# Moving rows between ScalarE and VectorE at the end of a load-bound clamp-and-sum kernel

## The chip, the cores and the metric

One core of a Trainium2 chip. The time of a kernel is the device time of one execution in microseconds (us); medians of several executions are given. Every execution also has a *span*: from the first to the last instruction that the profile records.

## The reference

```python
# x: (32, 512, 1024) float32
def reference(x):
    relu_x = np.maximum(x, 0)
    return np.sum(relu_x, axis=-1).astype(np.float32)
```

It reads 67.1 MB and writes 64 KB.

## The kernel before

The input is 16,384 rows of 1024 numbers, or 128 rows on each of the 128 partitions. It is loaded in seven blocks of 16 rows per partition, then 8, 4, 2 and 1 rows, and the last row in four pieces. Three buffers take turns. SyncE issues all loads on one queue. A row can be done in two ways:

- in two steps: ScalarE clamps several rows in one instruction in place, VectorE sums them in one instruction (`TWO` lists the group sizes of each block);
- whole: one engine clamps and sums one row (`ACT` and `DVE` count such rows). A whole row takes *two* hardware instructions, the work and a read of the accumulator.

```python
TWO = [[16], [16], [16], [8, 8], [8, 8], [6, 5], []]
ACT = [0, 0, 0, 0, 0, 5, 8]
DVE = [0, 0, 0, 0, 0, 0, 8]
TAIL = [8, 4, 2, 1]
PIECES = [244, 252, 260, 268]
# ...
    for j in range(NB):                       # the seven blocks
        buf = bufs[j % NBUF]
        loaded = load(buf[:, :, :], rows(m, ROWS), j >= NBUF and freed[j - NBUF])
        # ... clamp and total for n in TWO[j]; act_row x ACT[j]; dve_row x DVE[j]
        freed.append((n_act, n_dve))
    # the tail of 8, 4, 2, 1 rows goes into the buffer of the fifth block
    # ...
    for n in TAIL:
        loaded = load(buf[:, c : c + n, :], rows(m, n), None if c else freed[NB - NBUF])
        for i in range(n):
            if i % 2 == 0:
                act_row(buf[:, c, :], m, loaded if i == 0 else None)
            else:
                dve_row(buf[:, c, :], res[:, m : m + 1], loaded if i == 1 else None)
            # ...
    # ... then the four pieces of the last row on VectorE, and the stores
```

## Time and profile before

| | before |
|---|---|
| time, median of 3 | 163.16 us (163.13 to 163.45) |
| span of the profiled run | 160.7 us |
| that run's time less its span | 2.44 us |
| load queue, share of 16 engines' span | 97.6% |
| last piece of the input begins to be summed | 158.04 us |

The first fence holds the page's lines on the span, on busy time with instruction counts (x), and on the load queue (packets, MB, share of 16 DMA engines).

```profile
span 160.7 us, 162 instructions
## 1 busy us (share of the span) xinstructions
DVE 117.0 (73%) x47; ACT 102.8 (64%) x52; POOL 0.2 (0%) x4
...
q1 hardware_dynamic: 2592, 67.18, 97.6%
...
```

The queue is busy 97.6% of the span, while no compute engine is over 73%. The same in stretches of the run (columns: stretch, its length, busy time of VectorE, ScalarE and GpSimd with instruction counts, clock, DMA share, GB/s):

```profile
...
41.30:60.60 19.30, 17.18 (x2) 13.85 (x1) 0.00 (x0) 1.00 1.01 435
60.60:80.00 19.40, 17.26 (x2) 13.86 (x1) 0.00 (x0) 1.00 1.00 432
80.00:99.30 19.30, 19.30 (x2) 13.95 (x2) 0.00 (x0) 1.00 1.00 435
...
156.80:160.70 3.90, 1.63 (x8) 0.80 (x2) 0.00 (x0) 1.00 0.17 38
...
```

In full blocks the loads move 432 to 435 GB/s. The upper figure equals the fabric ceiling that the Trainium skill gives under "DMA: Bandwidth & Descriptors", Specifications, so moving rows between engines was not expected to hurry the stream. The last stretch, 3.9 us, holds the last of the pieces (38 GB/s over 3.9 us, about 0.15 MB) and what follows the stream.

The chain that ended last (start, length, what):

```profile
...
74.54 51.60 DVE res L119 x5
...
127.97 28.83 DMA piece<-in_x_dram
...
156.82 1.20 DVE piece L136 x6
...
158.04 0.44 DVE piece L204
...
```

The chain goes through 51.6 us of VectorE's sums, because they free the buffer that the tail is loaded into. This can be read as a trap. The loads that were released at 126 us stand in the queue behind a block that lands only at 138 us, and their data arrives in its turn; releasing them a little sooner or later should change nothing. The end of the chain is real: the last piece's data, then 0.44 us of VectorE, then a store.

VectorE's timeline of the tail (start, length, instruction, and in brackets the idle time before it and what ended it) shows the landings, because VectorE starts at 147.77 and 152.67 when a load lands:

```profile
...
138.06 1.22 DVE L136 TENSOR_SCALAR_CACHE_REDUCE io<-io 128x1024 f32<-128x1024 f32 x1
...
147.77 1.22 DVE L136 TENSOR_SCALAR_CACHE_REDUCE io<-io 128x1024 f32<-128x1024 f32 x1 [0.51 <-DMA io<-in_x_dram]
...
152.67 1.22 DVE L136 TENSOR_SCALAR_CACHE_REDUCE io<-io 128x1024 f32<-128x1024 f32 x1 [0.25 <-DMA io<-in_x_dram]
...
155.15 1.22 DVE L136 TENSOR_SCALAR_CACHE_REDUCE io<-io 128x1024 f32<-128x1024 f32 x1
...
156.82 0.41 DVE L136 TENSOR_SCALAR_CACHE_REDUCE piece<-piece 128x244 f32<-128x244 f32 x1 [0.44 <-DMA piece<-in_x_dram]
...
158.04 0.44 DVE L204 TENSOR_SCALAR_CACHE_REDUCE piece<-piece 128x271 f32<-128x271 f32 x1
...
```

Last, the groups by shape, from which the change is costed (busy time, then mean ns of one):

```profile
...
L119 DVE TENSOR_REDUCE res<-io 128x6 f32<-128x6144 f32 x1 | 6.5, 6546 | 0.0
L119 DVE TENSOR_REDUCE res<-io 128x5 f32<-128x5120 f32 x1 | 5.5, 5480 | 0.0
L111 ACT ACTIVATE io<-io 128x6144 f32<-128x6144 f32 x1 | 5.3, 5322 | 5.4 <-DMA io<-in_x_dram 5.4
L111 ACT ACTIVATE io<-io 128x5120 f32<-128x5120 f32 x1 | 4.5, 4453 | 0.0
...
L136 DVE DVE_READ_ACCUMULATOR io<-io 128x1 f32 x15 | 1.2, 82 | 0.0
...
```

One row costs 1066 ns in a sum, 6546 - 5480, and 869 ns in a clamp, 5322 - 4453. A whole row takes 1.14 us from start to start on VectorE, 1.04 us on ScalarE.

### The profile page before, as it was taken

Reading aid. Unit: us, or ns where it says so; the run is one execution under the profiler, and the core shown is the slowest. Engines: PE = TensorE matmul, PEld = TensorE weight load, DVE = VectorE, ACT = ScalarE, POOL = GpSimd, SP = SyncE. Lnnn points to the kernel's source line nnn. Section 1 sums busy time; section 2 is a strip of 40 time slices with the busy share of each in tenths; the row PEclk is TensorE's granted clock in tenths of the full one; section 3 lists DMA queues with packets and bytes.
Section 4 is the critical chain, followed back from the end, with each engine's and each line's share of the span. In section 5 each row is a group of like instructions: output and inputs, shape, how many; then the busy total and the mean of one; then the engine's idle time right before and its main releaser. Section 6 shows DMA issues by size and latency. Waiting matters only on the chain.

```text
span 160.7 us, 162 instructions
## 1 busy us (share of the span) xinstructions
DVE 117.0 (73%) x47; ACT 102.8 (64%) x52; POOL 0.2 (0%) x4
## 2 busy tenths in 40 slices
DVE  0000000009999499994999999999999999998984
ACT  3000059990799709995099932999249992696882
POOL 0000000000000000000000000000000000000000
DMA  7996996996996996996996996996996997998992
GB/s 261 522 522 261 522 522 261 522 522 261 522 522 261 522 522 261 522 506 277 522 489 294 522 489 294 522 489 294 522 489 294 522 440 343 392 481 371 424 389 47
DMA packets 2592, 67.18 MB, mean 418 GB/s; under 512 B 672, under 2 KB 1184, under 8 KB 1312
## 3 DMA queue, kind: packets, MB, share of 16 engines
q1 hardware_dynamic: 2592, 67.18, 97.6%
HBM read 67.11 MB, written 0.07 MB: 418 GB/s over the span
## 4 chain that ended last, share of the span: by engine, by line
DMA 43%; DVE 33%; ACT 17%; another core or an unknown queue 3%; SPq 1%; issue 0%; DVEq 0%
DVE res L119 32%; DMA io<-in_x_dram 25%; DMA piece<-in_x_dram 18%; ACT io L111 17%; SPq L93 1%; DVE piece L136 1%; DVE piece L204 0%; DVEq L29 0%
## 5 line engine op out<-in xcount | busy, mean ns | idle before, releaser
L119 DVE TENSOR_REDUCE res<-io 128x8 f32<-128x8192 f32 (+3 forms) x9 | 97.9, 10933 | 40.1 <-ACT io L111 40.1
L111 ACT ACTIVATE io<-io 128x8192 f32<-128x8192 f32 (+3 forms) x9 | 79.2, 8826 | 47.2 <-DMA io<-in_x_dram 47.2
L126 ACT ACTIVATE io<-io 128x1024 f32<-128x1024 f32 x21 | 21.9, 1044 | 6.8 <-DMA io<-in_x_dram 6.8
L136 DVE TENSOR_SCALAR_CACHE_REDUCE io<-io 128x1024 f32<-128x1024 f32 x15 | 17.4, 1215 | 0.9 <-DMA io<-in_x_dram 0.8
L126 ACT ACTIVATION_READ_ACCUMULATOR io<-io 128x1 f32 x21 | 3.9, 187 | 0.0
L111 ACT ACT_TABLE_LOAD x1 | 1.3, 1283 | 0.8 <-PEq L249 0.8
L136 DVE TENSOR_SCALAR_CACHE_REDUCE piece<-piece 128x244 f32<-128x244 f32 (+2 forms) x3 | 1.2, 416 | 0.4 <-DMA piece<-in_x_dram 0.4
L136 DVE DVE_READ_ACCUMULATOR io<-io 128x1 f32 x15 | 1.2, 82 | 0.0
L204 DVE TENSOR_SCALAR_CACHE_REDUCE piece<-piece 128x271 f32<-128x271 f32 x1 | 0.4, 436 | 0.0
L136 DVE DVE_READ_ACCUMULATOR piece<-piece 128x1 f32 x3 | 0.2, 82 | 0.0
L249 POOL MEMSET const-bfloat16-1.0<- 128x1 bf16 x1 | 0.1, 102 | 0.0
L249 POOL MEMSET const-uint8-127<- 128x1 uint8 x1 | 0.1, 101 | 0.0
L249 POOL MEMSET const-float32-0.0<- 128x1 f32 x1 | 0.1, 99 | 0.2 <-issue 0.2
L249 POOL MEMSET const-float32-1.0<- 128x1 f32 x1 | 0.1, 98 | 0.0
L204 DVE DVE_READ_ACCUMULATOR piece<-piece 128x1 f32 x1 | 0.1, 84 | 0.0
## 6 DMA issues: line engine op xcount, KB each, us to landing
io<-in_x_dram SPq DMA_DIRECT2D x1, 4096.0 KB, 21.6
io<-in_x_dram SPq DMA_DIRECT2D x1, 2048.0 KB, 26.1
io<-in_x_dram SPq DMA_DIRECT2D x1, 1024.0 KB, 28.1
io<-in_x_dram SPq DMA_DIRECT2D x1, 512.0 KB, 28.9
piece<-in_x_dram SPq DMA_DIRECT2D x1, 134.0 KB, 28.4
piece<-in_x_dram SPq DMA_DIRECT2D x1, 130.0 KB, 28.6
piece<-in_x_dram SPq DMA_DIRECT2D x1, 126.0 KB, 28.7
piece<-in_x_dram SPq DMA_DIRECT2D x1, 122.0 KB, 28.8
```

Of the source, the lines that this page charges most:

```text
L93: dma = nc.sync.dma_start(out=dst, in_=src)
L111: i = nc.scalar.activation(out=ap, in_=ap, func=RELU)
L119: nc.vector.tensor_reduce(out=res[:, m : m + n], in_=ap, axis=mybir.AxisListType.X, op=ADD).wait_op(sems.act, n_act, "sem-ge").then_inc(se ...
L126: i = nc.scalar.activation(out=ap, in_=ap, func=RELU, accum_out=res[:, m : m + 1])
L136: i = nc.vector.tensor_scalar(out=ap, in0=ap, scalar1=0.0, scalar2=None, op0=MAX, op1=ADD, accum_out=accum_out,)
L204: nc.vector.tensor_scalar(out=last[:, :], in0=last[:, :], scalar1=0.0, scalar2=None, op0=MAX, op1=ADD, accum_out=res[:, NT - 1 : NT],).wai ...
L249: nc = _bacc.Bacc("TRN2", target_bir_lowering=False, num_devices=1)
```

## The change

Its intent is to use ScalarE's and VectorE's idle time near the end in another proportion. The sixth block becomes 7 + 7 rows in two steps and 2 rows on ScalarE (was 6 + 5 and 5). Of the seventh, ScalarE takes 9 rows and VectorE 7 (was 8 and 8). Of the tail's eight rows ScalarE takes 5 and VectorE 3 (was 4 and 4). No load, store, buffer or release changes.

```diff
-TWO = [[16], [16], [16], [8, 8], [8, 8], [6, 5], []]
-ACT = [0, 0, 0, 0, 0, 5, 8]
-DVE = [0, 0, 0, 0, 0, 0, 8]
+TWO = [[16], [16], [16], [8, 8], [8, 8], [7, 7], []]
+ACT = [0, 0, 0, 0, 0, 2, 9]
+DVE = [0, 0, 0, 0, 0, 0, 7]
@@
-            if i % 2 == 0:
+            if i % 2 == 0 or (n == 8 and i == 7):
                 act_row(buf[:, c, :], m, loaded if i == 0 else None)
```

## The prediction

> **What bounds the kernel.** The stream of loads. The queue table gives q1 97.6% of 16 engines' span. The stage windows give 435 GB/s in the stretches 41.3 to 60.6 us and 80.0 to 99.3 us, and the timeline shows each full block (8.4 MB) landing 19.36 us after the one before: 99.34, 118.70, 138.06 us. The last nine loads then land in order of issue: 8 rows at 147.77, 4 at 152.67, 2 at 155.15, 1 at 156.45, pieces from 156.8. That 435 equals the fabric ceiling in the Trainium skill, "DMA: Bandwidth & Descriptors", Specifications; this trace agrees. After the last landing come four short VectorE instructions on the pieces (156.82 to 158.48) and a store of 1.4 us.
>
> The chain of waits names VectorE's sums for 33% and ScalarE's clamps for 17%. I read this as an artefact: those sums release buffers, but the queue never ran dry. The eight-row load was issued at about 126.2 us, when the previous block had 12 us of transfer left.
>
> **What changes.** Sixth block: 11 rows clamped and summed plus 5 whole rows on ScalarE become 14 plus 2. Seventh: ScalarE 8 to 9 rows, VectorE 8 to 7. In the next eight rows: ScalarE 4 to 5, VectorE 4 to 3. No load, store, buffer or release changes: the last buffer that is used again is freed by the fifth block's sums, which are untouched. The queue's instruction list is the same.
>
> **Costs, from the groups by shape.** Sums: 6546 ns for 6 rows and 5480 for 5, so 1066 per row and an estimated 7.61 us for 7. Clamps: 5322 and 4453, so about 6.18 us for 7. A whole row takes 1.14 us start to start on VectorE and 1.04 on ScalarE.
>
> VectorE: sums start at 126.04 as before; two of 7 rows end near 141.2 instead of 137.98. It meets the seventh block 3.1 us late; seven rows end near 149.1 (147.3 before), so it is 1.3 us late for the eight rows that land at 147.77. Three rows there end at about 152.5 to 152.6, just ahead of the landing at 152.67. Caught up, by some 0.1 us.
>
> ScalarE: its clamps and two rows end near 133.1, ahead of the landing at 138.06. Nine rows end near 147.5, before 147.77. Five rows end near 153.0, 0.3 us late for the four-row load, two more near 155.15: caught up.
>
> Busy time should be VectorE 117.0 to about 117.6 us and ScalarE 102.8 to about 104.1. Nothing on the path of load stream, last piece and last store changes.
>
> **Prediction.** 163.15 us, 8 in 10 between 162.8 and 163.5. Faster by over 2%: 1%; within 2%: 98%; slower: 1%.
>
> **What the profile would show.** Right: landings at 138.06, 147.77, 152.67, 155.15, 156.45 and 156.8 within 0.1 us; queue share near 97.6%; VectorE without idle time from 74.5 us until about 152.5 us, its first row of the seventh block near 141.1; ScalarE idle from 133.1 to 138.06; first piece at 156.82 and the span near 160.7.
> Wrong: the pieces' sums starting later than their landing (VectorE's debt not paid); or landings that shift (engine work affects the transfers).
>
> **What would make it wrong.** VectorE's debt when the four-row load lands would have to exceed about 0.6 us (its idle time after that: 0.2 + 0.4) to reach the pieces: sums or rows slower than measured here. So would another rate of the loads; nothing here points to it.

## The result, and the profile after

The median fell to 162.59 us (162.49 to 162.68, 4 runs), beside 163.14 for the kernel before in the same comparison. The ratio is 0.9964, with a 95% interval of 0.9946 to 0.9981. Ratios are the mean time of one kernel's runs over that of the other's of the same rounds, so not quite the ratio of the medians. So it is a gain of about a third of a per cent: within 2%, as forecast, but outside the range of 162.8 to 163.5, and clear of noise.

The page of the kernel after:

```profile
span 160.7 us, 156 instructions
## 1 busy us (share of the span) xinstructions
DVE 117.7 (73%) x43; ACT 104.2 (65%) x50; POOL 0.2 (0%) x4
...
q1 hardware_dynamic: 2592, 67.18, 97.5%
...
```

The span is 160.7 us again, to the digit, with the same queue share. The instruction counts fell: 162 to 156 in all, VectorE 47 to 43, ScalarE 52 to 50. The chain:

```profile
...
74.57 51.60 DVE res L119 x5
...
128.01 28.82 DMA piece<-in_x_dram
...
156.86 1.15 DVE piece L136 x6
...
158.06 0.43 DVE piece L204
...
```

The same chain with the same lengths. VectorE's timeline:

```profile
...
141.13 1.21 DVE L136 TENSOR_SCALAR_CACHE_REDUCE io<-io 128x1024 f32<-128x1024 f32 x1
...
149.11 1.21 DVE L136 TENSOR_SCALAR_CACHE_REDUCE io<-io 128x1024 f32<-128x1024 f32 x1
...
152.53 0.08 DVE L136 DVE_READ_ACCUMULATOR io<-io 128x1 f32 x1
152.70 1.22 DVE L136 TENSOR_SCALAR_CACHE_REDUCE io<-io 128x1024 f32<-128x1024 f32 x1
...
155.19 1.22 DVE L136 TENSOR_SCALAR_CACHE_REDUCE io<-io 128x1024 f32<-128x1024 f32 x1
...
156.86 0.41 DVE L136 TENSOR_SCALAR_CACHE_REDUCE piece<-piece 128x244 f32<-128x244 f32 x1 [0.43 <-DMA piece<-in_x_dram]
...
158.06 0.43 DVE L204 TENSOR_SCALAR_CACHE_REDUCE piece<-piece 128x271 f32<-128x271 f32 x1
...
```

VectorE comes to the seventh block at 141.13 instead of 138.06, is late for the eight rows of the tail (149.11 instead of 147.77), has caught up at 152.70, and meets the pieces at 156.86 as before (156.82). Everything the prediction said of the span happened. And yet the time is 0.5 us shorter. Where is it?

Each execution has its own time and span. Time less span was 2.44 us in the profiled run of before, and 1.92 to 1.99 us (mean 1.96) in the four runs of after. So nearly the whole difference lies *outside the span*: after the last instruction that the profile records, or before the first.

One more thing differs in the trace. Besides the loads and stores it holds some DMA records of the kind "instruction", 8192 bytes each. The trace's page does not list them; these, read from the kept trace itself, are the records, with start times from the span's start:

```
8192-byte records of kind "instruction", profiled runs (start in us, from the span's start)
before  -11.03 -10.98 -10.82 -9.34 -8.42 -8.35 -8.13   and 162.81 (2.11 us after the span's end)
after   -11.02  -9.10  -8.40 -8.39 -8.30
```

I take such a record for the fetch of a block of instructions; the trace gives only its kind and size. The kernel before has one 2.1 us after its span, the kernel after has none. This gave the theory to test.

### The profile page after: what moved, and what is told of

The parts are those of the page before. It is cut to its first block, busy times and chain, and to the rows that moved or that the text cites. A ratio compares the mean times of both kernels' runs of the same rounds, so it can differ in the third digit from the quotient of the medians. Undisturbed runs are those within 1.5% of the kernel's fastest.

```text
span 160.7 us, 156 instructions
## 1 busy us (share of the span) xinstructions
DVE 117.7 (73%) x43; ACT 104.2 (65%) x50; POOL 0.2 (0%) x4
## 3 DMA queue, kind: packets, MB, share of 16 engines
q1 hardware_dynamic: 2592, 67.18, 97.5%
## 4 chain that ended last, share of the span: by engine, by line
DMA 43%; DVE 33%; ACT 17%; another core or an unknown queue 3%; SPq 1%; issue 0%; DVEq 0%
DVE res L119 32%; DMA io<-in_x_dram 25%; DMA piece<-in_x_dram 18%; ACT io L111 17%; SPq L93 1%; DVE piece L136 1%; DVE piece L204 0%; DVEq L29 0%
## 5 line engine op out<-in xcount | busy, mean ns | idle before, releaser
L119 DVE TENSOR_REDUCE res<-io 128x8 f32<-128x8192 f32 (+2 forms) x9 | 101.1, 11287 | 40.1 <-ACT io L111 40.1
L111 ACT ACTIVATE io<-io 128x8192 f32<-128x8192 f32 (+2 forms) x9 | 81.7, 9110 | 47.2 <-DMA io<-in_x_dram 47.2
L126 ACT ACTIVATE io<-io 128x1024 f32<-128x1024 f32 x20 | 20.8, 1043 | 5.4 <-DMA io<-in_x_dram 5.3
L136 DVE TENSOR_SCALAR_CACHE_REDUCE io<-io 128x1024 f32<-128x1024 f32 x13 | 15.0, 1214 | 0.2
```

What stands on the lines that cost most here:

```text
L111: i = nc.scalar.activation(out=ap, in_=ap, func=RELU)
L119: nc.vector.tensor_reduce(out=res[:, m : m + n], in_=ap, axis=mybir.AxisListType.X, op=ADD).wait_op(sems.act, n_act, "sem-ge").then_inc(se ...
L126: i = nc.scalar.activation(out=ap, in_=ap, func=RELU, accum_out=res[:, m : m + 1])
L136: i = nc.vector.tensor_scalar(out=ap, in0=ap, scalar1=0.0, scalar2=None, op0=MAX, op1=ADD, accum_out=accum_out,)
```

## Experiments

**Theories.** *Lengths*: the time outside the span depends on how many instructions ScalarE's and VectorE's streams hold, whatever they do. *Division* (the rival): it is the new division of rows among the engines. *Build*: each build of a program, or each chip, falls where it falls, and the 0.5 us is luck. The texts before each run use letters: A and V are *Lengths* of ScalarE's stream alone and of VectorE's alone, L of both together; S and W are *Division*; N is *Build*; B and C, explained where they come up, are two ideas of how the lengths act.

Stream lengths below are counted in the compiled programs (in every run 4 more for each of the two engines than its trace lists), and are written (ScalarE, VectorE): the kernel before is (62, 58), after is (60, 54). Streams were lengthened with drains, instructions that do no work, at the head of an engine's list, where ScalarE waits 19.9 us and VectorE 35.8 us for the first data:

```diff
+    for _ in range(2):
+        nc.scalar.drain()
+    for _ in range(4):
+        nc.vector.drain()
     freed = []
     m = 0
     for j in range(NB):
```

All outputs are right. In the text that follows, "outside" is the mean of time less span over a kernel's runs. The kernel before had 2.35 us outside over its 43 runs below (2.11 to 2.49).

### Is it one of the two streams, or one part of the change?

Two kernels pad one stream of the kernel after to before's length; two others apply one part of the change to the kernel before.

`a_act2`: after, 2 drains for ScalarE (62, 54).

> The kernel after, with two idle instructions (drains) put at the head of ScalarE's list, where it waits 19.9 us for the first block anyway: ScalarE's instruction stream is as long as before (62, not 60), VectorE's stays at 54. Its work, tiles and loads are those of the kernel after. Theory A (the 0.5 us lies outside the span and depends on the length of ScalarE's stream): 163.1 us, time less span 2.4 us. Theory V (the same, of VectorE's stream): 162.6 us, time less span 1.95. Theory S (the division of the last blocks among the engines itself): 162.6. Theory N (each build of a program falls where it falls): anything.

Measured: 162.69 us, outside 1.87, ratio 0.9982 (0.996 to 1.0003).

`a_dve4`: after, 4 drains for VectorE (60, 58).

> The kernel after, with four drains at the head of VectorE's list, where it waits 35.8 us: VectorE's stream is as long as before (58, not 54), ScalarE's stays at 60. Theory V: 163.1 us, time less span 2.4. Theory A: 162.6 us, time less span 1.95. Theory S: 162.6. Theory N: anything.

Measured: 162.74 us, outside 2.03, ratio 0.9986 (0.9962 to 1.001). Neither stream alone brings back before's 2.35. Theories A and V as worded both fall.

`b_sixth`: before, with the first part alone (56, 58).

```diff
-TWO = [[16], [16], [16], [8, 8], [8, 8], [6, 5], []]
-ACT = [0, 0, 0, 0, 0, 5, 8]
+TWO = [[16], [16], [16], [8, 8], [8, 8], [7, 7], []]
+ACT = [0, 0, 0, 0, 0, 2, 8]
```

> The kernel before with the first part of the change alone: sixth block 7 + 7 rows clamped and summed and 2 on ScalarE; seventh 8 and 8, tail 4 and 4 as before. ScalarE's stream falls to 56, VectorE's stays at 58. Worked out from the durations: VectorE starts the seventh block near 141.1, ends its eight rows near 150.2, its four tail rows near 154.8 (2.1 us after the four-row load lands), then three rows to about 158.2 and the four pieces to about 159.9 instead of 158.5: span longer by about 1.3 us. Theory A: time less span 1.95, total near 163.9 to 164.0. Theory V: time less span 2.4, total near 164.4.

Measured: 164.00 us, ratio 1.006 (1.004 to 1.008), outside 2.07, mean span 161.93. Here the span itself grew, for the reason worked out in advance. VectorE's timeline:

```profile
...
140.95 1.21 DVE L136 TENSOR_SCALAR_CACHE_REDUCE io<-io 128x1024 f32<-128x1024 f32 x1
...
156.90 1.22 DVE L136 TENSOR_SCALAR_CACHE_REDUCE io<-io 128x1024 f32<-128x1024 f32 x1
...
158.04 0.40 DVE L136 TENSOR_SCALAR_CACHE_REDUCE piece<-piece 128x244 f32<-128x244 f32 x1
...
159.16 0.43 DVE L204 TENSOR_SCALAR_CACHE_REDUCE piece<-piece 128x271 f32<-128x271 f32 x1
...
```

From 140.95 us on VectorE works without a pause to the end, meets the pieces at 158.04 where the kernel before met them at 156.82, and the last one at 159.16 instead of 158.04: 1.12 us late. So the other two parts of the change are what pays for the first. (Its total of 164.0 happens to agree with theory A's figure, but `a_act2` had refuted theory A beside it.)

`b_rest`: before, with the other two parts alone (66, 54).

```diff
-ACT = [0, 0, 0, 0, 0, 5, 8]
-DVE = [0, 0, 0, 0, 0, 0, 8]
+ACT = [0, 0, 0, 0, 0, 5, 9]
+DVE = [0, 0, 0, 0, 0, 0, 7]
@@
-            if i % 2 == 0:
+            if i % 2 == 0 or (n == 8 and i == 7):
```

> The kernel before with the other two parts alone: seventh block 9 rows on ScalarE and 7 on VectorE, tail of eight 5 and 3; sixth block as before. ScalarE's stream grows to 66, VectorE's falls to 54. Both engines keep up with the landings, so the span stays near 160.7. Theory A: time less span 2.4, total 163.1. Theory V: time less span 1.95, total 162.6. Theory S (relieving VectorE late is what counts): 162.6 or less, with a shorter span.

Measured: 162.44 us, ratio 0.9963 (0.9943 to 0.9983), span 160.65, outside 1.77. These two parts alone give as much as the whole change. The sixth block's part is not needed.

### Is it luck? Is it the lengths together?

`null_before`: the kernel before against itself (62, 58).

> The kernel before, word for word, measured as if it were a changed one against itself. If the procedure has no bias, ratio 1.000 within 0.001, span 160.7, time less span spread over 2.1 to 2.4 us as the seven runs of before of the last call. If a program's first place in the procedure or its build decides (theory N), its time less span differs from that of the runs of before beside it, for instance 1.9.

Measured: 163.09 us beside 163.09, ratio 0.9998 (0.9985 to 1.0012), outside 2.34. No bias.

`rep_after`: the kernel after again (60, 54).

> The kernel after, word for word, again. If the 0.5 us belongs to the program: ratio near 0.997, span 160.7, time less span 1.9 to 2.0. If it belonged to that one build or that chip (theory N): ratio anywhere from 0.996 to 1.002.

Measured: 162.69 us, ratio 0.9972 (0.9959 to 0.9984), outside 1.94. The gain belongs to the program: theory *build* falls. In size it is a little under the first 0.55 us: 0.40 us between the medians here, and 0.46 in `rep_after2` below.

`a_both`: after, with both streams at before's lengths (62, 58), by the edit shown above.

> The kernel after with two drains at the head of ScalarE's list and four at the head of VectorE's: both instruction streams are as long as before (62 and 58) while the work is that of the kernel after. Theory L (lengths of the two streams together, where neither alone did it): 163.0 us, time less span 2.2 to 2.4. Theory W (what the engines do, not how long their lists are): 162.6, time less span 1.9 to 2.0.

Measured: 163.09 us beside 163.09, ratio 0.9997 (0.9985 to 1.001), span 160.70, outside 2.38. This is the deciding run: the work, tiles and division of the kernel after, with six idle instructions at the very start, has the time of the kernel before. An instruction record is back at 162.97 us, 2.15 us after the span's end.

`a_big`: after, 32 drains on each list (92, 86).

> The kernel after with 32 drains at the head of each of the two lists (streams of 92 and 86 instructions), still inside the engines' wait for the first block. If time outside the span grows with the length of a stream, it must show here: 30 instructions more than before, so well over 2.4 us. If it does not depend on the length: 1.9 to 2.0 us and 162.6.

Measured: 163.25 us, ratio 1.0006 (0.9993 to 1.0018), outside 1.78, span 161.44. So the time outside does *not* grow with the length; with much longer streams it is the shortest of all. But two instruction records now lie inside the run, at 122.49 and 142.29 us, and the span is longer. ScalarE's timeline of the kernel after shows when the sixth and the seventh block and the tail's eight rows land:

```profile
...
118.74 12.24 ACT L111 ACTIVATE io<-io 128x7168 f32<-128x7168 f32 x2 [5.40 <-DMA io<-in_x_dram]
...
138.09 1.06 ACT L126 ACTIVATE io<-io 128x1024 f32<-128x1024 f32 x1 [5.03 <-DMA io<-in_x_dram]
...
147.81 1.06 ACT L126 ACTIVATE io<-io 128x1024 f32<-128x1024 f32 x1 [0.26 <-DMA io<-in_x_dram]
...
```

And of this kernel:

```profile
...
118.62 12.24 ACT L111 ACTIVATE io<-io 128x7168 f32<-128x7168 f32 x2 [5.40 <-DMA io<-in_x_dram]
...
138.15 1.06 ACT L126 ACTIVATE io<-io 128x1024 f32<-128x1024 f32 x1 [5.21 <-DMA io<-in_x_dram]
...
148.62 1.06 ACT L126 ACTIVATE io<-io 128x1024 f32<-128x1024 f32 x1 [1.00 <-DMA io<-in_x_dram]
...
```

From the seventh block to the eight rows it is 9.72 us in the kernel after and 10.47 here, 0.75 more, in the interval that holds the record at 142.29 (325 ns long). In the other 19 profiles the same two loads land 9.71 to 9.86 us apart. The interval before it, which holds the record at 122.49, is longer by only 0.18 (138.15 - 118.62 against 138.09 - 118.74); intervals between full blocks vary as much where no record lies inside (19.59 in `a_act6b`), so this one shows nothing. VectorE then sees the four rows 0.82 us and the pieces 0.77 us later than in the kernel after:

```profile
...
153.52 1.22 DVE L136 TENSOR_SCALAR_CACHE_REDUCE io<-io 128x1024 f32<-128x1024 f32 x1 [1.02 <-DMA io<-in_x_dram]
...
157.63 0.41 DVE L136 TENSOR_SCALAR_CACHE_REDUCE piece<-piece 128x244 f32<-128x244 f32 x1 [0.39 <-DMA piece<-in_x_dram]
...
```

So the load stream was delayed in the interval of the second record, and `a_72_66` below has the same at another place; why by more than the record's own 0.3 us is not settled.

### Where are the thresholds?

`L66_58`: after, 6 and 4 drains.

> The kernel after with 6 drains for ScalarE and 4 for VectorE: streams of 66 and 58 (before: 62 and 58, time less span 2.4; 66 and 54 gave 1.77). Theory C (the 0.4 us is a collision: both engines fetch their next block of instructions at the same moment after the span, and the second waits): 66 fetches earlier, no collision, time less span 1.8 to 2.1, 162.5 to 162.7. Theory B (VectorE's late fetch costs when ScalarE has passed a threshold of 61 or 62): 2.4, total 163.1. A growth with length: over 2.4.

Measured: 162.81 us, ratio 0.9982 (0.9958 to 1.0006), outside 2.07, with a record 1.03 us after the span. Theory B falls; C is kept for the moment.

`L62_62`: after, 2 and 8 drains.

> The kernel after with 2 drains for ScalarE and 8 for VectorE: streams of 62 and 62. Theory C: VectorE fetches earlier, no collision, time less span 1.8 to 2.1. A mirror of theory B (ScalarE's late fetch costs when VectorE has passed a threshold between 55 and 58): 2.4. A growth with length: over 2.4.

Measured: 163.01 us, ratio 0.9991 (0.9969 to 1.0013), outside 2.34, a record 2.10 us after the span. Theory C foretold 1.8 to 2.1, and misses: a longer VectorE stream did not take the coincidence away. The mirror of theory B (ScalarE's late fetch costs once VectorE's stream is past a threshold) foretold 2.4 and fits; no later run refutes it, and none tests it further.

`L61_58`: after, 1 and 4 drains.

> The kernel after with 1 drain for ScalarE and 4 for VectorE: streams of 61 and 58, one instruction of ScalarE less than before. 60 and 58 gave 2.02. A threshold at 62: 2.0. A threshold at 61: 2.4. A smooth growth: in between, 2.2.

Measured: 163.10 us, ratio 1.0 (0.9974 to 1.0027), outside 2.43, against 2.03 at (60, 58). One idle instruction, 0.4 us: a step, not a slope.

`L62_56`: after, 2 and 2 drains.

> The kernel after with 2 drains for ScalarE and 2 for VectorE: streams of 62 and 56; 62 and 54 gave 1.86, 62 and 58 2.4. A threshold at 57 or 58: 1.9. At 55 or 56: 2.4. A smooth growth: 2.1.

Measured: 162.58 us, ratio 0.9968 (0.9942 to 0.9993), outside 1.89. VectorE's step lies above 56.

### Does it hold for before's own work?

`b_act4`: before, plus 4 drains for ScalarE (66, 58), nothing removed.

> The kernel before with four drains added at the head of ScalarE's list, nothing taken away: streams of 66 and 58. If the lengths alone decide: time less span 2.05 as for the kernel after at 66 and 58, total 162.7 to 162.8, so 0.3 us faster than before by adding instructions. If the division of rows decides: 163.1, time less span 2.4.

Measured: 162.69 us, ratio 0.9977 (0.9964 to 0.9989), span 160.66, outside 2.08. *Adding* four instructions made the kernel before faster by 0.4 us. No theory of work or of its division can say that; the lengths foretold it, to 0.03 us outside the span.

`a_act6`: after, 6 drains for ScalarE (66, 54).

> The kernel after with six drains at the head of ScalarE's list: streams of 66 and 54. If the lengths alone decide: time less span 1.75 to 1.8 as for before's sixth block at 66 and 54, total 162.45, the fastest so far beside that one. If that one was fast for its sixth block: 1.9 to 2.0, 162.6.

Measured: 162.60 us, ratio 0.9972 (0.9958 to 0.9985), outside 1.80, equal to `b_rest` with the other division (1.77) at the same lengths. The total missed the 162.45, because the spans came out longer (160.80 in the mean against 160.65).

`a_72_66`: after, 12 drains on each list.

> The kernel after with 12 drains on each list: streams of 72 and 66. With 92 and 86 the time outside was 1.78 but the two fetches fell inside the load stream and the span grew by 0.6 to 0.8. If both fetches now fall just after or near the end of the span: time less span 1.75 to 1.8 with a span of 160.7, 162.45. If VectorE's fetch falls inside the load stream: span 161.0 or more.

Measured: 162.85 us, ratio 0.9983 (0.9971 to 0.9996), outside 1.83, mean span 161.02. One record lies inside the load stream again, at 151.75 us, and the span is 0.3 longer. The two loads around it, the eight and the four rows, land 5.27 us apart, against 4.85 to 4.91 in the other profiles.

`b_one`: before, with `[6, 5]` made `[11]` (61, 57).

> The kernel before with the sixth block's two pairs made one (11 rows clamped, then 11 summed): streams of 61 and 57, one instruction less on each engine. VectorE waits about 2.1 us for the larger clamp and is some 0.3 us late at the pieces: span 160.7 to 160.9. VectorE's threshold at 57: time less span 2.4, total 163.1 to 163.3. At 58: 1.9, total 162.6 to 162.8.

Measured: 162.79 us, ratio 0.998 (0.9968 to 0.9993), mean span 161.02 (160.7 to 160.9 was expected), outside 1.78. So 57 is below VectorE's step and 58 above it.

### Does any version beat both?

`rep_after2` and `a_act6b`: the kernel after, and the same with six drains for ScalarE, side by side.

> The kernel after, a third time: time less span 1.9 to 2.0, total 162.6 to 162.7, ratio to before 0.9970.

> The kernel after with six drains for ScalarE, word for word as a_act6, beside the kernel after on the same chip. If its advantage outside the span is real: time less span 1.75 to 1.85, total 0.1 to 0.2 us under the kernel after's of this call. If it was the call: no difference.

Measured: 162.61 us, ratio 0.9979 (0.9964 to 0.9993), outside 1.95; and 162.67 us, ratio 0.9972 (0.9961 to 0.9984), outside 1.77. The 0.18 us outside the span is repeatable, but the spans scatter by more from run to run (160.6 to 161.3), and the totals cannot be told apart. No run here clearly beats the kernel after.

### All lengths together

| (ScalarE, VectorE) | kernels | outside, us | late instruction record, us after the span |
|---|---|---|---|
| (60, 54) | after, `rep_after`, `rep_after2` | 1.94 to 1.96 | none |
| (62, 54), (62, 56) | `a_act2`, `L62_56` | 1.87, 1.89 | none |
| (61, 57) | `b_one` | 1.78 | none |
| (66, 54) | `b_rest`, `a_act6`, `a_act6b` | 1.77 to 1.80 | 1.0 to 1.1 |
| (92, 86), (72, 66) | `a_big`, `a_72_66` | 1.78, 1.83 | none; 1.2 |
| (56, 58), (60, 58) | `b_sixth`, `a_dve4` | 2.07, 2.03 | none |
| (66, 58) | `L66_58`, `b_act4` | 2.07, 2.08 | 1.03, 1.27 |
| (61, 58), (62, 58), (62, 62) | before, `null_before`, `a_both`, `L61_58`, `L62_62` | 2.34 to 2.43 | 2.1 to 2.2 in four of five profiles |

Every kernel with VectorE at 57 or less has 1.96 us or less outside. With VectorE at 58 it is 2.0 to 2.1 when ScalarE is at 56, 60 or 66, and with VectorE at 58 or 62 and ScalarE at 61 or 62 it is 2.3 to 2.4. Longer is not slower: (92, 86) is among the shortest, and (66, 58) lies under (62, 58).

That the lengths decide is shown, from both sides (`a_both`, `b_act4`). All drains stood at the head of a list, so whether the number of instructions counts or where the list ends in memory was not separated.

Does the late fetch cost the time? No run isolates it, but the kept traces say more than the table. They also hold updates of semaphores, the counters by which engines signal each other. The last update comes 1.90 to 2.05 us after the span in all 20 profiles, whether 1.78 or 2.44 us lie outside. So up to that update the runs are alike to 0.15 us, and the larger differences lie elsewhere: after it, or before the span. In the four profiles with a record over 2 us after the span, the time outside (here with the trace's exact span) follows the *end* of that record, which speaks for the end:

| | record's length, us | record's end, us after the span | outside, us | record's end less outside, us |
|---|---|---|---|---|
| before | 0.57 | 2.67 | 2.44 | 0.23 |
| `a_both` | 0.36 | 2.51 | 2.28 | 0.23 |
| `L61_58` | 0.43 | 2.61 | 2.38 | 0.23 |
| `L62_62` | 0.57 | 2.67 | 2.44 | 0.23 |

(The record ends after the measured time would if that began with the span. Where the measured time begins is not recorded, so only that the difference stays the same counts.) The one profile of (62, 58) without such a record, that of `null_before`, has 2.14, the lowest of that kernel's five runs. And the records that start at 1.0 to 1.3 us end before the last update; at (66, 54), with one, 1.77 to 1.80 us lie outside, as in `b_one` (1.78), without one. So the late fetch is supported, on four profiles, as what ends these runs late; it is not shown by a run that changes it alone. Open are which engine fetches, why these lengths put the fetch there, and why four profiles without a record over 2 us (`b_sixth`, `L66_58`, `b_act4`, `null_before`) end about 0.28 us later after the last update than the eight shortest.

## Why the prediction was right or wrong

Point by point:

- *The load stream bounds the kernel, and moving rows does not touch it.* Right. Span 160.7 and 160.7, queue share 97.6% and 97.5%, landings 0.03 to 0.04 us apart.
- *The chain of waits is an artefact where it names the sums.* Right as far as the change tests it: the chain kept its 51.60 us.
- *VectorE is 3.1 us late at the seventh block and has caught up before 152.67.* Right. It started at 141.13 (141.1 foretold) and ended the tail's third row at 152.61 (152.5 to 152.6 foretold). `b_sixth` shows the limit: without the rows handed to ScalarE it is not caught up, and the pieces start 1.22 us late.
- *Busy time 117.6 and 104.1 us.* 117.7 and 104.2.
- *163.15 us, 162.8 to 163.5.* Wrong, by 0.56 us. The step that failed is the unspoken one from "Nothing on the path of load stream, last piece and last store changes" to the time. The sum was span plus what lies outside it. The first term was right. The second was in effect carried over at the 2.44 us of the profiled run, as a constant (2.35 is its mean over 43 runs), and measured 1.96. It was never examined, although time (163.14) and span (160.7) stood side by side, and although the change takes instructions out of both lists: two whole rows of VectorE's among them, at two instructions each.
- *What would make it wrong: VectorE's debt, or another rate of the loads.* Neither happened. The one term that moved was not in the list.

The gain is therefore not what the change meant to do. Its division of rows is worth nothing here: at equal stream lengths, (62, 58), it has the time of the kernel before (ratio 0.9997). It gains because the lengths of the two streams changed, from (62, 58) to (60, 54): the two rows taken from VectorE held two instructions each, and ScalarE has one whole row less. Either part alone keeps most of what is gained outside the span: 1.87 us at (62, 54) and 2.03 at (60, 58), against 2.35 before and 1.96 after. Behind this stands, on the evidence of four profiles, a late instruction fetch that the three profiles of (60, 54) do not hold.

## What to carry to other kernels

When a forecast says "same" because all the work moves inside slack, check the part of the time that the span does not hold: subtract the span from the time of each run, before and after. Where effects of 0.3% matter, count the instructions of each engine's stream as well as their durations, and test a suspected effect of the count with idle instructions at a place where the engine waits anyway: that separates the length of a program from its work. And do not read a small gain as a proof of the idea behind the change; here one part of it, alone, cost 0.6%, and the gain came from a side effect.

## What the Trainium skill lacked or had wrong

- "Runtime: NRT & Kernel Launch", The ~15µs preamble/postamble breakdown, gives fixed times for what surrounds a kernel and names engine count and DMA setup as what varies the total. Here the time outside the span took values from 1.77 to 2.43 us for the same work and the same engines, in steps, by the lengths of two instruction streams; one instruction of ScalarE made 0.4 us.
- The same page, Instruction fetch mechanics, says that instruction memory is refilled in 16 KiB blocks. All records of the kind "instruction" longer than 24 bytes in these traces are of 8192 bytes, and those late in the run come singly. Whether a block is smaller than stated or is fetched in parts is not shown.
- The same section says that the cost of crossing a block boundary is "mostly hidden". If these records are such crossings, it was not hidden here: where one fell inside the load stream, the next load landed later by about 0.4 us (`a_72_66`) and 0.75 us (`a_big`), and the mean span grew by 0.3 us (`a_72_66`, one record) and 0.7 us (`a_big`, two).
- "DMA: Bandwidth & Descriptors", Specifications: the ceiling of 435 GB/s agrees with the 432 to 435 measured. No page gives a figure for what an instruction fetch costs a load stream at that ceiling; the delays just given are the two that these runs show.
